# Head weights in pairs, a later load of y and later gated products in a hybrid S5 and attention block

## The chip, the core and the metric

The kernel runs on one core of a Trainium2 chip. The metric is the device time of one execution in microseconds (us). The engines work side by side, each through its own list of instructions in order: PE (TensorE, matrix products; PEld are its weight loads), DVE (VectorE), ACT (ScalarE), POOL (GpSimd), and SP (SyncE), which here issues nearly all transfers. An engine that waits for one instruction holds everything behind it.

## The reference

One decoder block over 1024 tokens of width 1024, in float32. What matters here is the first part: one normalised input `u` is projected to the input of a state-space branch, to queries, keys and values of 8 attention heads of width 64, to forget logits and to gates.

```python
u = rms_norm(h, norm_mix[l])
proj = u @ w_in[l]
u_ssm, q, k, v, f_logit, gate_logits = jnp.split(proj, [...], axis=-1)
y_ssm = jax.nn.gelu(s5_ssm(u_ssm, ...))
glu_a, glu_b = jnp.split(y_ssm @ w_glu[l], 2, axis=-1)
out_a = glu_a * jax.nn.sigmoid(glu_b)
att = forgetting_attention(q, k, v, f_logit + b_forget[l])   # causal, biased by summed log f
out_b = att @ w_fox_o[l]
h = h + (gate_a * out_a + gate_b * out_b) @ w_mix_out[l]
```

A cross-attention into 256 memory tokens, a gated FFN and a final norm follow.

## The kernel before

**Precision and stages.** Every float32 operand of a product is split into a high and a low part: ACT casts (`split`, line 178), DVE subtracts (line 179), and PE runs three products per tile pair (`mm3`, lines 168 to 170). The stages are the input with the norm, the state-space branch with the gates, the attention (class `Fox`), and the tail with the rest of the block. The attention stage runs from about 317 to 610 us and holds all of the change.

**Heads.** `Fox.run` loops over 8 heads and, in each, over 12 units: pairs of a block of 512 queries and a tile of 128 keys, numbered 0 to 11, units 0 to 3 for the first block and 4 to 11 for the second. `scores` issues a unit's products, the exponential on ACT (line 1627), and the split of the probabilities on ACT and DVE, or on DVE and POOL; `values_hi` and `values_lo` follow some units later. When the last unit of a head is summed, the first units of the next are under way: then `finish` fetches the head's denominators (`rc`, line 1663), DVE takes the reciprocals, and they go through DRAM (line 1665) and come back spread over 64 partitions (`rb`, line 1667). This last transfer is `self.spread`. `divide`, called in unit 4 of the next head, multiplies by it on DVE (line 1673), splits the result and stores it.

**Work beside the units.** `side[i]` lists what is issued with unit i of head h: in units 0 to 11 the projection of head h+2 (`part`, with the copies out of PSUM in `evac`), the row maxima of head h+1 (`row_max`, with `max_row` in unit 9, which sends the row by line 1610), the load of head h+3's query and key weights in unit 5 and their split in unit 9. In head 6 the y tiles, the output of the state-space branch, are loaded from DRAM (`load_y`: 8 calls of two transfers of 256 KB). In head 7 the `filler` is issued: loads of GLU weights and products with y, `Glu.values` for four blocks of 128 output columns.

**Buffers and order.** All weight loads, of the heads, of the GLU and of the later output projection, go through two buffers called `raw`, and their halves through four buffers each of `whi` and `wlo`. `raw` is free again when ACT and DVE have split it. The program order above is not the final one: a scheduler that models times moves instructions on each engine, so GLU weight loads (line 153) are issued on SP well ahead of head 7, from 506 us on, and loads of y (line 1698) from 526 us on, in head 5. `issue_after`, and `behind` on top of it, keep instructions from moving ahead of a named one. The GLU weights are first copied to `wg_d` in another order (line 1713).

**Pieces.** One head's queries take 64 columns of `w_in`, so a load of them consists of runs of 64 floats, 256 bytes.

Of the kernel before, what the change touches and what calls it, by code (L numbers as in the profile page):

```python
# [9 lines left out]
F32 = mybir.dt.float32  # L10
F32R = mybir.dt.float32r
# [8 lines left out]
P = 128  # L20
D = 1024
# [3 lines left out]
NH = 8  # L25
DH = 64
# [5 lines left out]
RAW = 1072  # L32

WSLOT = 1088
# [15 lines left out]
C_U, C_Q, C_K, C_V, C_G = 0, 512, 1024, 1536, 2056  # L50
# [16 lines left out]
def f32(ap):  # L67
    return ap.bitcast(F32)
# [26 lines left out]
def weave(main, side, lead=0):  # L95

    n, m, done = len(main) - lead, len(side), 0
    for i, f in enumerate(main):
        f()
        want = m if i + 1 == len(main) else max(0, (i + 1 - lead) * m // max(n, 1))  # L100
        while done < want:
            side[done]()
            done += 1
# [1315 lines left out]
class Fox:  # L1419
# [109 lines left out]
    def project(self, h):  # L1529

        B = self.B
        V, A, S = B.V, B.A, B.S
        K1, K2, Q1, Q2 = self.hb[h % 2]

        def load(behind=None):
            src = lambda c: self.w_in[:, c + h * DH:c + (h + 1) * DH].rearrange("(k p) c -> p k c", p=P)
            raw = self.raw[h] = B.wpool.tile([P, RAW], F32, tag="raw", bufs=2, name="raw")[:, :D]
            rv = raw.rearrange("p (k c) -> p k c", k=8)
            with B.behind(behind):
                S.dma_start(rv[:, :, 0:64], src(C_Q))  # L1540
                return S.dma_start(rv[:, :, 64:128], src(C_K))

        def parted(behind=None):
            wh = B.wpool.tile([P, WSLOT], F32R, tag="whi", name="whi")[:, :D]
            wl = B.wpool.tile([P, WSLOT], F32R, tag="wlo", name="wlo")[:, :D]
            with B.behind(behind):
                B.split(wh, wl, self.raw.pop(h))
            self.pj[h] = [t.rearrange("p (k c) -> p k c", k=8) for t in (wh, wl)]

        def part(hf, k):  # L1550
            if k == 0:
                self.pj[h, hf] = B.bank("mm")
            wh, wl = self.pj[h]
            rh, rl = self.uT.rhs(k, hf)
            B.mm3(self.pj[h, hf], wh[:, k, :], wl[:, k, :], rh, rl, k == 0, k == 7)

        def evac(hf):
            if hf == 1 and h > 1:
                self.gate_rows(h)
            ps = self.pj.pop((h, hf))  # L1560
            cs = slice(512 * hf, 512 * hf + 512)
            A.activation(Q1[0:64, cs], ps[0:64, :], AF.Copy, scale=0.125)
            A.copy(K1[0:64, cs], ps[64:128, :])
            V.scalar_tensor_tensor(out=Q2[64:128, cs], in0=ps[0:64, :], scalar=0.125, in1=f32(Q1[0:64, cs]),
                                   op0=ALU.mult, op1=ALU.subtract)
            V.tensor_sub(K2[0:64, cs], ps[64:128, :], f32(K1[0:64, cs]))
            A.activation(Q2[0:64, cs], ps[0:64, :], AF.Copy, scale=0.125)
            return A.copy(K2[64:128, cs], ps[64:128, :])

        return Projection(load, parted, [lambda hf=hf, k=k: part(hf, k) for hf in range(2) for k in range(8)],  # L1570
                          [lambda: evac(0), lambda: evac(1)])

# [113 lines left out]
    def run(self, y_d, yT, aT, w_glu, w_d, filler):  # L1686
        B, fp, S = self.B, self.fp, self.B.S
        self.aT = aT
        self.prepare_v()
        for t in range(NT):  # L1690
            self.values_of_v(1, t)
        self.log_forget()
        self.setup()

        def load_y(k, h):

            for i, dst in enumerate(yT.rhs(k, h)):
                S.dma_start(f32(dst).rearrange("p (t c) -> p t c", t=4),
                            y_d[k, i, 4 * h:4 * h + 4].rearrange("t p c -> p t c"))

        def load_att(k):
            for h in range(2):
                for i, dst in enumerate(aT.rhs(k, h)):
                    S.dma_start(f32(dst), self.att_d[i, k * P:(k + 1) * P, 512 * h:512 * h + 512])

        pro = [self.project(h) for h in range(NH)]
        for h in range(2):
            loaded = pro[h].load()
            pro[h].split()

        with B.tc.issue_after(loaded.ins):
            for k in range(4):
                S.dma_start(w_d[k].rearrange("(m g) c -> m g c", g=8),
                            w_glu[k * P:(k + 1) * P].rearrange("(g m) c -> m g c", m=16))
        for f in pro[0].parts[:8] + pro[0].evac[:1] + pro[0].parts[8:] + pro[0].evac[1:]:
            f()
        self.cumulate()
        for t in range(4):
            self.values_of_v(0, t)
        for h in range(2):  # L1720
            self.gate_rows(h)
        for f in pro[1].parts[:4]:
            f()
        weave(pro[1].parts[4:8] + pro[1].evac[:1] + pro[1].parts[8:], self.row_max(0))
        copied = pro[1].evac[1]()
        self.values_of_v(0, 4)
        self.max_row(0)
        pro[2].load()
        pro[2].split(copied)
        pro[3].load()  # L1730
        for t in range(5, 7):
            self.values_of_v(0, t)
        units = [(qc, kt) for qc in range(2) for kt in range(4 * qc + 4)]
        for h in range(NH):
            side = {i: [] for i in range(12)}
            late = h == NH - 2
            if late:
                for i, f in enumerate(pro[h + 1].parts[8:]):
                    side[i // 2].append(f)
                side[3].append(pro[h + 1].evac[1])  # L1740
            if h + 1 < NH:
                for i, f in enumerate(self.row_max(h + 1)):
                    side[(RSLOT_LATE if late else RSLOT)[i]].append(f)
                side[9].append(lambda: self.max_row(h + 1))
            if h + 2 < NH:
                n = 8 if h + 3 == NH else 16
                for i, f in enumerate(pro[h + 2].parts[:n]):
                    side[i if n == 8 else PSLOT[i]].append(f)
                side[9].append(pro[h + 2].evac[0])
                if n == 16:  # L1750
                    side[11].append(pro[h + 2].evac[1])
            if h + 3 < NH:
                side[9].append(lambda: pro[h + 3].split(self.exp))
            if h > 0 and h + 3 < NH:
                side[5].append(lambda: pro[h + 3].load(self.spread))
            if h == 0:
                side[0].append(lambda: self.values_of_v(0, 7))
            if late:
                for k in range(8):
                    side[4 + k].append(lambda k=k: load_y(k // 2, k % 2))  # L1760
            if h == NH - 1:
                for k in range(3):
                    side[6 + k].append(lambda k=k: load_att(k))
                for i, f in enumerate(filler):
                    side[i * 12 // len(filler)].append(f)
            for i, u in enumerate(units):
                self.scores(h, *u)
                for f in side[i]:
                    f()
                if len(self.hi_todo) > 2:  # L1770
                    self.values_hi()
                if len(self.lo_todo) > 1:
                    self.values_lo()
                if h and i == 4:
                    with B.tc.issue_after(self.mark.ins):
                        self.divide(h - 1)
        while self.hi_todo:
            self.values_hi()
        while self.lo_todo:
            self.values_lo()  # L1780
        self.divide(NH - 1)
# [29 lines left out]
```

## Time and profile before

| | us |
|---|---|
| median of 3 runs | 1593.38 (1593.16 to 1594.76) |
| the profiled execution | 1588.78 |
| its span | 1586.7 |

The mean granted clock of PE over the span was 0.988. A row of the timeline reads: start, duration, engine (`SPq` is SP issuing a transfer), line, operation, output<-input, sizes, and in brackets how long the engine stood before it and what ended that. In these rows raw<-in_w_in_dram in lines 1540 and 1541 is a head's load, raw<-wg_d a piece of GLU weights, yh and yl<-y_d a piece of y.

The wait list of PE between 300 and 680 us names ACT's `whi` (2.7 us, one time), ACT's exponentials (2.5 us, three times) and POOL's `pl` (1.5 us, one time) as the longest. From 580 us to 843 us no gap of PE above 0.2 us is in the trace.

### The profile page before, as it was taken

How to read it: one execution, taken by the hardware profiler on the slowest of the kernel's cores; microseconds unless marked ns; L12 is line 12 of the kernel's file. 1: busy time of each engine (PE TensorE's matmuls, PEld its weight loads, DVE VectorE, ACT ScalarE, POOL GpSimd, SP SyncE). 2: the span in 40 equal slices, each digit the busy share in tenths (PEclk: the TensorE clock that was granted, in tenths of full speed). 3: DMA queues.
4: the chain of work that ended last, by engine and by line, in shares of the span. 5: the costliest groups of instructions: out<-in, count | busy, mean ns of one | idle time of the engine just before them, and what ended most of it. 6: DMA issues, size and time to landing. Idle time of an engine off the chain costs nothing.

```text
span 1586.7 us, 20446 instructions
## 1 busy us (share of the span) xinstructions
PE 1534.0 (97%) x7313; PEld 1261.3 (79%) x7313; DVE 1019.5 (64%) x1850; ACT 655.2 (41%) x1173; POOL 254.3 (16%) x335
## 2 busy tenths in 40 slices
PE   7799999999999899999999999999999999999997
PEld 6578888898777668888888778888888888788885
DVE  6666445344688687675555697766677776565555
ACT  6422434323576553222435564333333333254342
POOL 2027653200212124110002200100000000000001
PEclk8899999999999999999999999999999999999999
DMA  7764445652023736357412186555444554796642
GB/s 266 125 132 80 127 131 110 130 145 30 18 52 48 186 95 208 125 172 259 160 46 75 54 283 239 170 164 163 155 153 160 166 162 156 261 391 223 195 150 106
DMA packets 197940, 240.86 MB, mean 152 GB/s; under 512 B 35448, under 2 KB 126488, under 8 KB 197328
## 3 DMA queue, kind: packets, MB, share of 16 engines
q1 hardware_dynamic: 191216, 223.84, 48.2%
q10 hardware_dynamic: 6624, 15.73, 2.6%
q8 instruction: 57, 0.93, 0.2%
q14 instruction: 43, 0.35, 0.1%
HBM read 165.60 MB, written 75.86 MB: 152 GB/s over the span
## 4 chain that ended last, share of the span: by engine, by line
PE 75%; DVE 8%; DMA 7%; issue 4%; POOL 3%; ACT 2%; SPq 1%; DVEq 0%; POOLq 0%; ACTq 0%
PE mm L868 14%; PE mm L168 7%; PE pv L868 7%; PE mm L170 7%; PE mm L169 7%; PE mm L1005 4%; PE sc L868 3%; PE sc L1005 3%; PE pv L1005 3%; PE sc L168 3%; PE sc L169 3%; PE sc L170 3%; DMA raw<-in_w_in_dram 2%; PE misc L1005 1%; PE pv L168 1%
## 5 line engine op out<-in xcount | busy, mean ns | idle before, releaser
L179 DVE TENSOR_TENSOR wlo<-raw,whi 128x1024 fp32r<-128x1024 f32 (+2 forms) x121 | 132.0, 1094 | 135.1 <-ACT whi L178 133.9
L178 ACT CAST whi<-raw 128x1024 fp32r<-128x1024 f32 (+2 forms) x124 | 116.1, 940 | 220.0 <-DMA raw<-in_w_ffn_in_dram 54.1
L168 PE MATMUL mm<-uh,whi 128*128 128x512 f32 x344 | 138.8, 404 | 2.8 <-ACT whi L178 2.7
L170 PE MATMUL mm<-uh,wlo 128*128 128x512 f32 x344 | 136.5, 397 | 1.7 <-DVE wlo L179 1.7
L169 PE MATMUL mm<-ul,whi 128*128 128x512 f32 x344 | 136.4, 396 | 0.0
L179 DVE TENSOR_TENSOR ol<-or,oh 128x1024 fp32r<-128x1024 f32 x73 | 89.3, 1224 | 71.6 <-ACT oh L178 70.3
L178 ACT CAST oh<-or 128x1024 fp32r<-128x1024 f32 x73 | 76.8, 1052 | 105.3 <-PE mm L1005 33.6
L900 POOL TENSOR_TENSOR g<-a,c 128x512 f32<-128x512 f32 x22 | 35.2, 1600 | 392.8 <-ACT a L899 373.9
L170 PEld LDWEIGHTS mm<-uh,wlo 128*128 128x128 f32 x344 | 65.7, 191 | 16.5 <-DVE wlo L179 3.1
L1630 POOL TENSOR_TENSOR pl<-pf,ph 128x512 fp32r<-128x512 f32 (+1 forms) x32 | 39.7, 1239 | 241.1 <-DVE ph L1629 196.1
L168 PEld LDWEIGHTS mm<-uh,whi 128*128 128x128 f32 x344 | 65.9, 192 | 15.5 <-ACT whi L178 3.2
L169 PEld LDWEIGHTS mm<-ul,whi 128*128 128x128 f32 x344 | 66.0, 192 | 11.3
L197 POOL TENSOR_TENSOR r<-ms,mhalf 128x1 f32<-128x1 f32 x26 | 15.1, 582 | 354.9 <-DVE ms L193 344.5
L1627 ACT ACTIVATE pf<-sc 128x512 f32<-128x512 f32 (+1 forms) x96 | 46.5, 490 | 46.3 <-DVE sc L1623 28.6
L868 PE MATMUL pv<-S3h,we 128*128 128x512 f32 x176 | 58.1, 389 | 0.0
L1633 DVE TENSOR_TENSOR pl<-pf,ph 128x512 fp32r<-128x512 f32 (+2 forms) x64 | 35.1, 550 | 10.2 <-ACT ph L1632 9.5
L1005 PE MATMUL mm<-oh 128*128 128x512 f32 x106 | 41.2, 389 | 0.0
L1005 PE MATMUL mm<-ol,oh 128*128 128x512 f32 x106 | 41.2, 389 | 0.0
L1005 PE MATMUL mm<-oh,ol 128*128 128x512 f32 x106 | 41.2, 389 | 0.0
L168 PE MATMUL mm<-yh,whi 128*128 128x512 f32 x104 | 40.9, 393 | 0.0
L168 PE MATMUL sc<-uh,whi 128*128 128x512 f32 x104 | 40.8, 393 | 0.0
L170 PE MATMUL mm<-yh,wlo 128*128 128x512 f32 x104 | 40.6, 390 | 0.0
(580 smaller groups left out, 4537.5 us busy)
## 6 DMA issues: line engine op xcount, KB each, us to landing
or<-c_d SPq DMA_DIRECT2D x77, 256.0 KB
raw<-in_w_in_dram SPq DMA_DIRECT2D x22, 512.0 KB
wo<-in_w_ffn_out_dram SPq DMA_DIRECT2D x22, 512.0 KB
c_d<-g SPq DMA_DIRECT2D x44, 256.0 KB
t_d<-wo SPq DMA_DIRECT2D x44, 256.0 KB
or<-t_d SPq DMA_DIRECT2D x44, 256.0 KB
raw<-in_w_ffn_in_dram SPq DMA_DIRECT2D x20, 512.0 KB
rawb<-in_w_ffn_in_dram SPq DMA_DIRECT2D x20, 512.0 KB
```

The source lines that it names most:

```text
L168: T.matmul(ps, lh, rh, start=first, stop=False)
L169: T.matmul(ps, lh, rl, start=False, stop=False)
L170: T.matmul(ps, ll, rh, start=False, stop=last)
L178: self.A.copy(hi, src)
L179: (self.G if pool_lo else self.V).tensor_sub(lo, src, f32(hi))
L197: self.G.tensor_tensor(out=r, in0=v, in1=self.mhalf[:, 0:n], op=ALU.pow)
L868: T.matmul(ps, l_[:, k, :], r_, start=first and k == 0 and i == 0, stop=k == 3 and i == 2, skip_group_check=True)
L900: G.tensor_mul(g[:, 512:], a1, c1)
L1005: T.matmul(ps, l_[:, gi], r_[:, 512:], start=n < 3 and p == 0 and k == 0 or n == 7 and p == 0 and k == 0, stop=p == NP - 1 and k == 2, ski ...
L1627: self.exp = A.activation(pf[:, off:], ps[:, off:], AF.Exp)
L1630: G.tensor_sub(pl[:, off:], pf[:, off:], f32(ph[:, off:]))
L1633: V.tensor_sub(pl[:, off:], pf[:, off:], f32(ph[:, off:]))
```

## The change

There are three parts. A head's query and key columns were loaded into one `raw` buffer by two transfers of 256-byte pieces. Now one load covers two heads: the queries of both into one buffer, the keys of both into the other, in 512-byte pieces, 512 KB each. Heads 0 and 1 are loaded at the start, 2 and 3 after the row maxima of head 0, 4 and 5 in unit 5 of head 1, 6 and 7 in unit 5 of head 3. The split takes each head's half out of both buffers, in two casts and two subtractions of 128x512 in place of one of 128x1024. The loads of y may not be issued before the latest `self.spread`. And the filler of head 7 begins in unit 2 instead of 0.

```diff
         def load(behind=None):
-            src = lambda c: self.w_in[:, c + h * DH:c + (h + 1) * DH].rearrange("(k p) c -> p k c", p=P)
-            raw = self.raw[h] = B.wpool.tile([P, RAW], F32, tag="raw", bufs=2, name="raw")[:, :D]
-            rv = raw.rearrange("p (k c) -> p k c", k=8)
+
+            self.raw[h // 2] = []
+            for c in (C_Q, C_K):
+                raw = B.wpool.tile([P, RAW], F32, tag="raw", bufs=2, name="raw")[:, :D].rearrange("p (k c) -> p k c", k=8)
+                self.raw[h // 2].append(raw)
+                with B.behind(behind):
+                    last = S.dma_start(raw, self.w_in[:, c + h * DH:c + (h + 2) * DH].rearrange("(k p) c -> p k c", p=P))
+            return last
+
+        def parted(behind=None):
+            self.pj[h] = [B.wpool.tile([P, WSLOT], F32R, tag=t_, name=t_)[:, :D].rearrange("p (k c) -> p k c", k=8)
+                          for t_ in ("whi", "wlo")]
+            o = h % 2 * DH
             with B.behind(behind):
-                S.dma_start(rv[:, :, 0:64], src(C_Q))
-                return S.dma_start(rv[:, :, 64:128], src(C_K))
-
-        def parted(behind=None):
-            wh = B.wpool.tile([P, WSLOT], F32R, tag="whi", name="whi")[:, :D]
-            wl = B.wpool.tile([P, WSLOT], F32R, tag="wlo", name="wlo")[:, :D]
-            with B.behind(behind):
-                B.split(wh, wl, self.raw.pop(h))
-            self.pj[h] = [t.rearrange("p (k c) -> p k c", k=8) for t in (wh, wl)]
+                for i, raw in enumerate(self.raw[h // 2]):
+                    B.split(*[t_[:, :, i * DH:(i + 1) * DH] for t_ in self.pj[h]], raw[:, :, o:o + DH])
...
             for i, dst in enumerate(yT.rhs(k, h)):
-                S.dma_start(f32(dst).rearrange("p (t c) -> p t c", t=4),
-                            y_d[k, i, 4 * h:4 * h + 4].rearrange("t p c -> p t c"))
+                with B.behind(self.spread):
+                    S.dma_start(f32(dst).rearrange("p (t c) -> p t c", t=4),
+                                y_d[k, i, 4 * h:4 * h + 4].rearrange("t p c -> p t c"))
...
+        loaded = pro[0].load()
         for h in range(2):
-            loaded = pro[h].load()
             pro[h].split()
...
         pro[2].split(copied)
-        pro[3].load()
...
-            if h > 0 and h + 3 < NH:
+            if h in (1, 3):
                 side[5].append(lambda: pro[h + 3].load(self.spread))
...
                 for i, f in enumerate(filler):
-                    side[i * 12 // len(filler)].append(f)
+                    side[2 + i * 10 // len(filler)].append(f)
```

In the changed kernel as scheduled, the GLU loads of the first four blocks are issued on SP between head 4 and the start of head 6, all y loads between the spread of head 5 and the denominators of head 6, and the first products with y keep their place in PE's list (unit 9 of head 6).

## The prediction

> **What bounds the kernel now.** I read the page first, then busy time in stretches of 20 us, then PE's timeline where PE was not full, then what released each gap.
>
> ```profile
> span 1586.7 us, 20446 instructions
> PE 1534.0 (97%) x7313; PEld 1261.3 (79%) x7313; DVE 1019.5 (64%) x1850; ACT 655.2 (41%) x1173; POOL 254.3 (16%) x335
> 350.00:360.00 10.00, 9.03 (x56) 7.50 (x55) 8.62 (x22) 4.55 (x8) 0.00 (x0) 1.00 0.03 10
> 480.00:500.00 20.00, 19.98 (x99) 15.09 (x96) 15.88 (x36) 13.56 (x25) 3.86 (x3) 1.00 0.40 67
> 520.00:540.00 20.00, 16.64 (x74) 12.39 (x75) 13.80 (x37) 12.71 (x25) 3.33 (x3) 0.91 0.61 168
> 540.00:560.00 20.00, 16.65 (x80) 11.29 (x79) 15.38 (x36) 13.04 (x26) 2.03 (x2) 1.00 0.72 182
> 560.00:580.00 20.00, 17.98 (x86) 12.77 (x84) 16.81 (x36) 10.67 (x20) 5.63 (x3) 1.00 0.44 119
> ```
>
> PE sets the pace: time is only won where PE stands or is throttled. The columns of a stretch are its length, then PE, weight loads, DVE, ACT and POOL, then clock, DMA share and GB/s. In the attention stage PE is full at head 3 (480 to 500), but loses 3.36, 3.35 and 2.02 us in 520 to 580 (heads 5 and 6), and 0.97 us in 350 to 360. These 9.7 us, and what the clock loses, are all that this change can win.
>
> ```profile
> 505.17 0.58 SPq L1540 DMA_DIRECT2D raw<-in_w_in_dram  x1
> 506.42 8.55 SPq L153 DMA_DIRECT2D raw<-wg_d  x2
> 521.54 1.04 ACT L178 CAST whi<-raw 128x1024 fp32r<-128x1024 f32 x1 [4.85 <-DMA raw<-in_w_in_dram]
> 522.64 0.50 PE L168 MATMUL mm<-uh,whi 128*128 128x512 f32 x1 [2.74 <-ACT whi L178]
> 523.90 0.50 PE L170 MATMUL mm<-uh,wlo 128*128 128x512 f32 x1 [0.53 <-DVE wlo L179]
> 524.58 0.33 PE L1645 MATMUL pv<-ph,vhi 128*65 128x256 f32 x1 [0.19 <-ACT ph L1632]
> 524.00:526.00 2.00, 1.81 (x7) 1.27 (x7) 1.67 (x4) 1.97 (x6) 0.00 (x0) 0.74 0.04 10
> 526.00:528.00 2.00, 2.00 (x8) 1.50 (x7) 1.70 (x4) 0.22 (x1) 0.00 (x0) 0.50 0.26 78
> 528.00:530.00 2.00, 2.00 (x10) 1.67 (x9) 0.44 (x2) 1.70 (x4) 0.00 (x0) 0.90 0.65 187
> 508.00:514.00 6.00, 6.00 (x29) 4.31 (x28) 5.71 (x11) 3.94 (x6) 1.29 (x1) 1.00 0.41 26
> ```
>
> The largest loss is one event. Head 7's weights were asked for at 505.17, two pieces of the GLU weights stood behind them, and from 508 to 514 the DMA engines moved only 26 GB/s. The weights landed near 521.5, 16 us after their issue; ACT, in order, waited 4.85 us, and PE lost 2.74 + 0.53 + 0.19 = 3.46 us. Then the clock fell: (0.26 + 0.50 + 0.10) x 2 us = 1.7 us more. **Together 5.2 us.**
>
> **The change part by part.** *Two heads in one load.* Heads 6 and 7 come together in head 3, heads 4 and 5 in head 1; the issue that was late is gone. Head 6's own load shows whether the earlier place holds twice the bytes.
>
> ```profile
> 480.36 0.58 SPq L1540 DMA_DIRECT2D raw<-in_w_in_dram  x1
> L178 ACT CAST whi<-raw x1: 1049/1049/1049, 491.9 to 491.9; 128x1024 fp32r<-128x1024 f32 x1
> q1 hardware_dynamic: 1277, 0.57, 87.8%
> q1 hardware_dynamic: 2087, 1.04, 90.2%
> ```
>
> From issue to cast there are 11.5 us. The last two rows are the DMA queue (packets, MB, share of 16 engines) in 481 to 486, where nearly all packets are 256-byte pieces of that load, and in 550 to 554, where they are 512-byte pieces of the GLU weights: 5 x 16 x 0.878 / 1277 = 55 ns a packet, against 4 x 16 x 0.902 / 2087 = 28 ns. One head has 2 x 128 x 8 = 2048 packets of 256 bytes, 2048 x 55 / 16 = 7.0 us; a pair has 2048 of 512 bytes, 2048 x 28 / 16 = 3.6 us. The pair should land near 486, nearly 6 us before its cast. Bounds: nothing won if head 7's cast meets another wait, 5.2 us at most. I take 5.0.
>
> The Trainium skill speaks against a price that falls with size: "DMA: Bandwidth & Descriptors", section "Why small descriptors are slow", gives a packet a fixed cost of about 3 cycles on top of its bytes (11 cycles at 256 bytes), by which 512 bytes would cost more per packet, an estimated 1.7 times. The trace disagrees, with 55 against 28 ns; by that rule the pair would take about 12 us and be slightly late at two casts, some 2 us off the gain.
>
> *The split in halves.* A cast and a subtraction of 128x1024 become two of 128x512 for each of 8 heads.
>
> ```profile
> 511.85 0.62 ACT L1632 CAST ph<-pf 128x512 fp32r<-128x512 f32 x1
> 522.62 1.22 DVE L179 TENSOR_TENSOR wlo<-raw,whi 128x1024 fp32r<-128x1024 f32 x1 [4.64 <-ACT whi L178]
> 531.30 0.68 DVE L1633 TENSOR_TENSOR pl<-pf,ph 128x512 fp32r<-128x512 f32 x1
> ```
>
> ACT: 2 x 0.62 - 1.04 = 0.2 us a head; DVE: 2 x 0.68 - 1.22 = 0.14. ACT and DVE have 6.4 and 4.1 us free in the 20 us of head 3 and hide it: zero. Bound without that cover: 8 x 0.2 = 1.6 us.
>
> *GLU pieces and raw slots.* Both raw buffers now hold a pair until its second head is split, so the first GLU piece waits on SP for head 7's split (cast at 516.7 or so). Queued behind it are the gate rows and the row of maxima for head 5, which in the old order wait for head 4's last scores, later than the split: no cost. But in the new order ACT casts GLU blocks 0 and 1 early in head 5, right after the exponential of its third unit, and three of their four pieces are issued behind the fetch of head 4's denominators.
>
> ```profile
> 529.60 0.54 SPq L1663 DMA_DIRECT2D rc<-num  x1
> 531.92 0.38 ACT L1627 ACTIVATE pf<-sc 128x256 f32<-128x256 f32 x1
> 548.81 2.08 SPq L153 DMA_DIRECT2D raw<-wg_d  x4
> ```
>
> That exponential ends 2.7 us after the fetch. Four pieces issued from 548.81 moved 1.04 MB by 554, so three need some 4.5 us: ACT waits 1 to 2 us, the exponential of the fourth unit behind it. PE has projections and maxima of other heads meanwhile; I charge 1.0 us (0 to 3).
>
> *y behind the spread.* Before, sixteen y pieces ran in head 5 from 526.20 on and slowed the spread of head 4's reciprocals.
>
> ```profile
> 526.20 0.39 SPq L1698 DMA_DIRECT2D yh<-y_d  x1
> 536.22 0.47 SPq L1667 DMA_DIRECT2D rb<-rd_d  x1
> 541.53 1.22 DVE L1673 TENSOR_TENSOR num<-num,rb 64x1024 f32<-64x1024 f32 x1 [1.60 <-DMA rb<-rd_d]
> 544.50 0.39 PE L1620 MATMUL sc<-hb,hb 69*128 69x256 f32 x1 [1.51 <-ACT pf L1627]
> 550.03 0.39 PE L1593 MATMUL mm<-hb,hb 68*128 68x256 f32 x1 [0.52 <-ACT hb L1568]
> ```
>
> The division stood 1.60 us on DVE, in front of everything, and PE 1.51, then 0.52 us near 550. Of these 2.0 us I take back 1.5 (0 to 2.0), since three GLU pieces now run ahead of that spread. The other 1.3 us of 540 to 560 stand at the start of head 6, where ACT has two GLU casts among its exponentials; one remains there: 0.7 (0 to 1.3).
>
> The price is paid in head 6. y is now issued only behind head 5's spread, and PE's new order puts the first y products at the same place as before, in unit 9 of head 6, not two units later: the scheduler moves them up to where it expects y.
>
> ```profile
> 560.79 0.46 SPq L1667 DMA_DIRECT2D rb<-rd_d  x1
> 566.90 0.50 PE L168 MATMUL mm<-yh,whi 128*128 128x512 f32 x1
> q1 hardware_dynamic: 3962, 2.11, 99.4%
> 574.92 0.44 PE L1652 MATMUL pv<-pl,vhi 128*65 128x512 f32 x1 [1.52 <-POOL pl L1630]
> ```
>
> PE reaches them 6.1 us after that spread's issue, and needs six pieces (y blocks 0 and 1) within 2 us. The queue row is 532 to 540: 2.11 MB in 8 us, 264 GB/s, or 1.0 us for a piece of 0.26 MB. With about 2 us to the first byte, the spread itself and one GLU piece ahead, the second piece lands 6 us after the issue, the sixth 10, against a need at 6 to 8. In the new order reciprocal and spread also stand behind the split of a GLU block, about 1 us later. PE should wait 2 to 3 us in bits; I take 2.5 (0 to 6). The later pieces stand behind the stores of head 5's result on SP, but their products are spread over 574 to 583: no further cost. Of the 1.9 us that PE lost at 573 to 578 to POOL and DVE I take 1.0 back, since these engines catch up while PE waits.
>
> *Forget gate.*
>
> ```profile
> 355.60 0.60 PE L1498 MATMUL misc<-ident,logf 128*8 128x128 f32 x4 [0.55 <-DVE logf L1485]
> 357.57 0.60 PE L1498 MATMUL misc<-ident,logf 128*8 128x128 f32 x4 [0.42 <-DVE cum L1499]
> ```
>
> The new loads let the scheduler put these transposes some 48 matmuls later, about 5 us, so both waits (0.97 us) go; the gate rows come later too, still ahead of their first use near 378. I take 0.8 (-1 to 1).
>
> Sum: 5.0 - 1.0 + 1.5 + 0.7 - 2.5 + 1.0 + 0.8 = **5.5 us won**. The profiled execution took 1588.8 us (span 1586.7 plus 2.1 around it), so 1583.3 there. The runs shown have a median of 1593.4, 4.6 us above it; taking the same difference off, 1587.9.
>
> **The rivals.**
> *The wait only changes its place (1591).* ACT stands for the GLU pieces in head 5 as it stood for head 7's weights. For: the same queue, the same in-order ACT, two casts in a row. Against: the pieces are 512 bytes, and the wait is 1 to 2 us against 4.85. If PE loses the full 3 us of the bound and y costs 3, 3.0 remain of the gain: 1590.4 to 1591.
> *y is late (slower, 1598).* The mechanism is SP: the spread, and with it y, stands behind two GLU pieces, the first of which waits for a raw slot. In the row at 506.42 two such pieces held SP for 8.55 us. If SP is held so long ahead of head 5's spread, PE pays each us of it, and a gap above 2.74 us brings the clock's 1.7: 8.55 + 1.7 - 5.5 = 4.8 us slower. It decides from a slip of 3.8 us on. For: the spread does stand behind two pieces. Against: no 256-byte load is in flight there.
> *The pair is late.* If a packet cost by its bytes, 110 ns, a pair would take 14 us and miss two casts by about 3 us each: 1594. The 28 ns speak against it.
> *All waits go (1582).* y is in time and the casts don't wait: 5.2 + 2.0 + 1.3 + 1.9 + 1.0 = 11.4. For: each gap has its cause in a queue that the change reorders. Against: y's margin is negative by the rows.
>
> **How the numbers follow.** The forecast has 0.50, with its own range 1584 to 1590.5; changed place 0.20; slower 0.13; pair late 0.03; all gone 0.14. What a measurement can tell is about 0.2%, 3.2 us: faster is below 1590.2, slower above 1596.6. Faster takes nearly all of the forecast, all of the best case and a little of the changed place: 0.63; slower the y case and a tail of others, 0.15; the rest, 0.22, is the same. The range, 1582 to 1595, reaches from the best case to where part of the y case is left out.
>
> **What would show it.** Right: no wait of ACT for raw near 517, full clock from 520 to 540, PE above 19 us in each 20 us of heads 4 and 5, a wait of PE on y from DMA in unit 9 of head 6 of 1 to 4 us in all, and no wait at the transposes of the forget gate. Wrong: a wait of ACT on the pair's loads in heads 1 and 3; a half clock in head 6 or 7; ACT idle above 3 us for a GLU piece in head 5; SP held for several us ahead of the spread of head 5.

## The result

The changed kernel takes 1599.18 us (median of 7, 1596.14 to 1600.62) against 1593.16 us before on the same chip, a ratio of 1.0036 with a 95% interval of 1.0024 to 1.0048: 0.36% slower by that ratio, 6.0 us by the two medians, where 5.5 us less were forecast. The profiled execution took 1600.62 us.

### The profile page after: what moved, and what is told of

It is laid out like the page before. It is cut to its first block, busy times and chain, and to the rows that moved or that the text cites. A ratio compares the mean times of both kernels' runs of the same rounds, so it can differ in the third digit from the quotient of the medians.

```text
span 1598.9 us, 20437 instructions
## 1 busy us (share of the span) xinstructions
PE 1539.4 (96%) x7313; PEld 1264.1 (79%) x7313; DVE 1019.7 (64%) x1858; ACT 656.3 (41%) x1181; POOL 254.7 (16%) x335
## 4 chain that ended last, share of the span: by engine, by line
PE 73%; DVE 9%; DMA 7%; issue 5%; POOL 3%; ACT 2%; SPq 1%; DVEq 0%; POOLq 0%; ACTq 0%
PE mm L868 15%; PE pv L868 7%; PE mm L168 6%; PE mm L169 6%; PE mm L170 6%; PE mm L1005 5%; PE sc L868 4%; PE sc L1005 4%; PE pv L1005 3%; PE sc L168 3%; PE sc L170 3%; PE sc L169 3%; DMA raw<-in_w_in_dram 2%; PE misc L1005 2%; DMA raw<-in_w_mem_kv_dram 1%
## 5 line engine op out<-in xcount | busy, mean ns | idle before, releaser
L179 DVE TENSOR_TENSOR wlo<-raw,whi 128x1024 fp32r<-128x1024 f32 (+1 forms) x129 | 134.1, 1044 | 135.5 <-ACT whi L178 130.7
L178 ACT CAST whi<-raw 128x1024 fp32r<-128x1024 f32 (+1 forms) x132 | 117.1, 895 | 223.1 <-DMA raw<-in_w_ffn_in_dram 53.2
L169 PEld LDWEIGHTS mm<-ul,whi 128*128 128x128 f32 x344 | 66.1, 192 | 11.4
L169 PE MATMUL mm<-yl,whi 128*128 128x512 f32 x104 | 41.0, 395 | 0.7 <-DMA yl<-y_d 0.7
L1100 POOL TENSOR_TENSOR sg<-sg,ga 128x512 f32<-128x512 f32 x16 | 29.9, 1891 | 72.6 <-DVE sg L1093 72.6
```

The source lines that it names most:

```text
L169: T.matmul(ps, lh, rl, start=False, stop=False)
L178: self.A.copy(hi, src)
L179: (self.G if pool_lo else self.V).tensor_sub(lo, src, f32(hi))
L1100: self.B.G.tensor_mul(self.out[j][:, cs], self.out[j][:, cs], ga)
```

## The profile after

The page, and busy time in stretches of 20 us as it was shown for the kernel before (length, then PE, weight loads, DVE, ACT, POOL, then clock, DMA share, GB/s). Line numbers are those of each run's own kernel, so a line that is L1593 before can be L1596 after. Three dots in a view stand for rows left out.

```profile
span 1598.9 us, 20437 instructions
PE 1539.4 (96%) x7313; PEld 1264.1 (79%) x7313; DVE 1019.7 (64%) x1858; ACT 656.3 (41%) x1181; POOL 254.7 (16%) x335
```

```profile
380.00:400.00 20.00, 16.12 (x81) 13.56 (x80) 9.87 (x28) 5.21 (x10) 0.00 (x0) 0.83 0.20 23
...
480.00:500.00 20.00, 20.00 (x99) 15.26 (x98) 16.15 (x41) 12.48 (x25) 3.75 (x4) 1.00 0.52 35
500.00:520.00 20.00, 16.56 (x78) 11.83 (x78) 12.30 (x37) 10.34 (x23) 2.89 (x3) 1.00 0.35 71
520.00:540.00 20.00, 19.94 (x98) 15.07 (x98) 15.19 (x36) 14.16 (x28) 2.57 (x2) 1.00 0.19 46
540.00:560.00 20.00, 17.23 (x78) 11.38 (x76) 18.04 (x44) 13.66 (x24) 4.63 (x4) 1.00 0.39 104
560.00:580.00 20.00, 17.45 (x79) 11.21 (x77) 17.32 (x39) 12.04 (x24) 3.31 (x3) 1.00 0.67 177
```

The stall of head 7's weights is gone: 520 to 540 is full, at full clock. Two new holes have opened ahead of it, at 380 to 400 (with the clock at 0.83) and at 500 to 520. The first, in the timeline, the two transfer queues and the clock:

```profile
371.32 1.02 SPq L1542 DMA_DIRECT2D raw<-in_w_in_dram  x2
372.60 0.35 SPq L1578 DMA_DIRECT2D hb<-cum_d  x1
...
375.70 2.10 SPq L1579 DMA_DIRECT2D hb<-cum_d  x1
...
384.04 1.64 PE L1596 MATMUL mm<-hb 68*128 68x128 f32 x4 [3.88 <-DMA hb<-cum_d]
```

```profile
q1 hardware_dynamic: 1130, 0.59, 88.1%
```

```profile
385.00:387.00 2.00, 2.00 (x6) 1.42 (x6) 1.66 (x6) 0.00 (x0) 0.00 (x0) 0.50 0.11 33
```

The load of heads 2 and 3 (1 MB) is issued right ahead of the four transfers of gate rows, 8 KB each. From 376 to 385 (the queue row: packets, MB, share of 16 engines) the DMA engines were 88% busy and moved 66 GB/s; the rows landed behind that, PE stood 3.88 us, and then ran at half clock. The second hole:

```profile
488.99 1.21 SPq L1542 DMA_DIRECT2D raw<-in_w_in_dram  x2
...
502.71 0.62 ACT L178 CAST whi<-raw 128x512 fp32r<-128x512 f32 x1 [1.92 <-DMA raw<-in_w_in_dram]
506.23 0.62 ACT L178 CAST whi<-raw 128x512 fp32r<-128x512 f32 x1 [2.90 <-DMA raw<-in_w_in_dram]
...
504.19 0.27 PE L1610 MATMUL misc<-ident,mc 128*8 128x128 f32 x1 [1.61 <-DVE mc L1608]
506.90 0.50 PE L168 MATMUL mm<-uh,whi 128*128 128x512 f32 x1 [1.14 <-ACT whi L178]
```

```profile
q1 hardware_dynamic: 695, 0.36, 101.5%
```

The pair of heads 6 and 7 was asked for at 488.99 and had landed only at 506, 17 us later (below, this slow phase of a load is called the crawl). ACT waited at both casts; DVE's subtractions behind them held the row maxima (L1608), and PE lost 1.61 us to those and 1.14 us to the weights. The queue row is 492 to 500: 695 packets in 8 us, 87 per us, each 8 x 16 x 1.015 / 695 = 187 ns. (The share adds up the time of all packets that began in the window, so it can pass 100%.)

The starts of PE's instructions show where whole kernels differ, also where single gaps are too short to be listed. For each matrix instruction I took the time to the next one's start, less the 10th percentile of that time for the same operation, tiles and shape over all kernels here, and summed it over the same stretch of PE's list. Every kernel has the same 7313 matrix instructions, and a stretch holds the same ones in all of them, but for one at an edge. Stretches are named by their times in the profile of before; each row is one profiled execution, in us lost:

```
                              350-395 395-485 485-515 515-530 530-590   whole
before                            5.1     5.7     1.7     6.3    10.7   101.8
after                            10.1     6.8     6.1     0.6    14.0   114.0
E5 after, once more               9.5     6.8     6.4     0.7    14.8   111.9
E1 gate rows first                6.9     6.8     6.4     0.7    13.2   109.9
E10 the same, once more           5.4     6.8     6.1     0.7    13.7   104.2
E2 pairs only                     9.9     6.8     6.0     0.7    12.6   107.5
E6 gate rows first, old y         5.3     6.8     7.5     0.7    10.9   105.6
E12 as E6, later filler           6.6     6.8     6.6     0.6    11.2   102.9
E11 as E6, y held                 6.9     6.8     6.4     0.7    13.3   106.7
E3 y and filler only              6.7     5.6     1.6     6.9    14.2   108.8
E4 pair 6, 7 earlier             10.4    18.1     3.2     0.6    13.6   117.5
E7 head 7 behind head 6           6.5     5.7     7.3     0.5    12.5   106.2
E8 columns of pairs exchanged     9.4    10.7     2.0     0.7    14.8   111.8
E13 columns of heads exchanged    6.4     5.8     4.3     0.5    11.7   102.4
E9 head 7 in halves               6.7     5.6     1.7     0.5    12.8    98.8
```

From before to after: 5.0 us lost at the gate rows, 1.1 in heads 0 to 2, 4.4 at the pair, 5.7 won at head 7's stall, 3.3 lost in heads 5 and 6; 8.1 us in these stretches. The whole differs by 12.2 us, as the two spans do (1598.9 and 1586.7). The other 4.1 us lie outside these stretches, where both kernels run the same instructions and where two executions of one kernel (after and E5) differ by up to 2.7 us in a single stretch of 100 us. The execution of before that was profiled was one of its faster ones inside the stretches too: E7, E9 and E13, which do the same work at the gate rows and in heads 5 and 6, lose 6.4 to 6.7 and 11.7 to 12.8 us there. Against their means (6.5 and 12.3) the change loses 3.6 us at the gate rows and 1.7 in heads 5 and 6, which makes 5.1 us in all, near the 6.0 of the medians.

## The experiments

Every kernel was timed beside the kernel before on its chip; ratios are against that. The theory: (A) most is lost by the gate rows behind a 1 MB load, (B) the rest by the late pair of heads 6 and 7. The rival: y behind the spread.

**E1, gate rows first.** `gate_rows` returns its last transfer, and

```diff
-            self.gate_rows(h)
+            gates = self.gate_rows(h)
...
-        pro[2].load()
+        pro[2].load(gates)
```

> The changed kernel, but the load of heads 2 and 3 may not be issued ahead of the four transfers of gate rows of heads 0 and 1. Theory A (most of the loss is the gate rows standing behind a 1 MB load that crawls at some 50 GB/s, with the half clock that follows the wait): no wait of PE for cum_d above 1 us, full clock from 380 to 400, some 5 to 7 us less than the changed kernel, so 1592 to 1594, about the kernel before. Theory B (the loss lies with the pair of heads 6 and 7 and in heads 5 and 6): under 2 us less, 1597 to 1599. If the load of heads 2 and 3 then lands too late for head 2's cast, a new wait of ACT for raw appears near 385 to 395 and the gain is halved.

1594.76 us (median of 5), ratio 1.0035 (1.0022 to 1.0049). Its timeline at the place:

```profile
371.62 0.22 SPq L1578 DMA_DIRECT2D hb<-cum_d  x1
...
372.87 1.02 SPq L1542 DMA_DIRECT2D raw<-in_w_in_dram  x2
...
380.24 0.44 PE L1596 MATMUL mm<-hb 68*128 68x384 f32 x1 [0.81 <-ACT hb L1571]
```

The wait of 3.88 us is gone (0.81 us for another cause stands in its place, as before the change), with the bytes of the load unchanged: A's mechanism is there. But the 5 to 7 us that theory A expected did not show in the time: the ratio did not move against the 1.0036 of the changed kernel, which had been timed on another chip. So the size needed more runs (E5, E6, E10).

**E2, pairs only.** In the changed kernel:

```diff
-                with B.behind(self.spread):
+                with B.behind(None):
...
-                    side[2 + i * 10 // len(filler)].append(f)
+                    side[i * 12 // len(filler)].append(f)
```

> The kernel before with the loads in pairs alone: y is not held behind the spread and the filler begins in unit 0. If the pairs carry the loss (A and B together): both the wait of 3.9 us for cum_d and the wait for the pair of heads 6 and 7 are there, and the time is 1598 to 1602. If y behind the spread or the later filler carries it: 1590 to 1594.

1595.97 us (6 runs), ratio 1.0040 (1.0026 to 1.0055). The time lies between the two ranges expected, but the kernel before was faster on this chip (1590.27 us), and by the ratio the pairs alone make the kernel slower by as much as the whole change. Both waits are there, 3.9 us for the gate rows and up to 2.6 us of ACT for the pair.

**E3, y and filler only**: these two hunks the other way round, in the kernel before.

> The kernel before with y behind the spread and the filler two units later, the head loads one by one as before. If the pairs carry the loss: not slower than before, 1590 to 1594, with the stall of head 7's weights near 521 still there, and heads 5 and 6 changed by under 2 us. If y carries the loss: 1597 to 1600, with waits of PE on y of over 3 us in head 6.

1595.06 us (5 runs), ratio 1.0035 (1.0021 to 1.0048). Slower too, against what I expected: the two halves of the change each cost what both cost together. They can, since the pairs win the 5.7 us of head 7's stall and lose more elsewhere, while E3 keeps that stall (6.9 us in 515 to 530). Heads 5 and 6 lost 3.5 us more than before, not under 2, of which waits of PE on y are 0.8 us.

**E4, the pair of heads 6 and 7 earlier.**

```diff
-                side[5].append(lambda: pro[h + 3].load(self.spread))
+                side[5 if h == 1 else 0].append(lambda: pro[h + 3].load(self.spread if h == 1 else None))
```

> The changed kernel, but the load of heads 6 and 7 is asked for in unit 0 of head 3 and without the spread, so that its query half leaves as soon as a raw buffer is free. Theory B (17 us from issue to landing, two casts late, their DVE halves and the row of maxima late with them): no wait of ACT for raw near 503 and 506, PE above 19.7 of 20 us in 500 to 520, and 2.5 to 3.5 us less than the changed kernel, 1595.5 to 1597. Theory A alone: no change, 1599, since these waits would be hidden. The wait for cum_d near 384 stays in both.

1605.55 us (4 runs), ratio 1.0103 (1.0087 to 1.0119): far worse than either expectation. The scheduler issued the first half at 474.26, just ahead of the row of maxima of head 3:

```profile
474.26 0.39 SPq L1542 DMA_DIRECT2D raw<-in_w_in_dram  x1
475.14 0.71 SPq L1613 DMA_DIRECT2D hb<-mr  x1
...
488.84 0.80 PE L1623 MATMUL sc<-hb,hb 69*128 69x512 f32 x1 [9.73 <-DMA hb<-mr]
```

A row of 4 KB took over 13 us behind the load, and PE stood 9.73 us. The casts of the pair no longer waited (ACT's rows show no idle time ahead of them, and 485 to 515 lost 3.2 us, not 6.1), so B stands; but what such a load costs is set by the small transfers issued behind it. It is the gate rows' accident at another place.

**E5, the changed kernel once more.**

> The changed kernel itself once more, beside the kernel before and the next kernels. Single times of one kernel lie up to 8 us apart, so what a part costs is read against this run. Expected 1.0036 (1.0025 to 1.005) of the kernel before. The waits that the first trace shows (near 384 for cum_d, near 503 and 506 for the pair) must be there again; the places of half clock need not.

1597.67 us (6 runs), ratio 1.0037 (1.0023 to 1.0051). The waits are there again: 4.1 us of PE for the gate rows, 2.9 us and 2.3 us of ACT for the pair.

**E6, gate rows first, y and filler as before**: E1 and E2 together, beside E5.

> The pair loads with the gate rows ahead of the load of heads 2 and 3, and with y and the filler as before the change. Theory: two causes, each about half. The gate rows cost 4 to 5 us, y and filler 2 to 4, the late pair 4, and the stall of head 7 that is gone gives 5 back. Then this kernel comes to 1.000 of the kernel before (0.998 to 1.002). Rival (y and filler cost nothing, the earlier run's 4.8 us was chance of the clock): as the run with the gate rows first alone, 1.0035.

1592.74 us (12 runs), ratio 1.0006 (0.9992 to 1.0019): the first expectation. Against E2, each by the kernel before on its chip, the gate rows are worth about 0.34%, from runs on two chips.

**E10 to E12, y or filler.** On one chip: E1 again; E1 with the second hunk of E2 (y held, filler from unit 0); E1 with its first hunk (y not held, later filler).

> The first experiment once more, on one chip with the next two: the pair loads with the gate rows ahead, y and filler as changed. Earlier 1.0035, and 1.0006 with y and filler as before. If y and filler cost what that says: 1.002 to 1.0035. If the earlier figure was high by chance: 1.0005 to 1.0015.

> Gate rows ahead, pair loads, y behind the spread, filler from unit 0. If y behind the spread is what costs in heads 5 and 6 (waits of PE on y near 575, 1.5 to 2.5 us in all): as the run before this one, 1.002 to 1.0035. If the later filler costs: 1.0005, as with both undone.

> Gate rows ahead, pair loads, y not held, filler from unit 2. If y behind the spread is what costs: 1.0005, as with both undone. If the later filler costs: 1.002 to 1.0035.

E10: 1594.74 us (12 runs), ratio 1.0021 (1.0010 to 1.0033), so the first figure of this kernel, 1.0035, was on the high side. E11: 1593.62 us (11 runs), 1.0021 (1.0011 to 1.0031). E12: 1591.17 us (11 runs), 1.0001 (0.9991 to 1.0012). Holding y costs some 0.2%, about 3 us; the later filler nothing. The traces show most of it: 13.7 and 13.3 us lost in heads 5 and 6 with y held (E10, E11), 10.9 and 11.2 without (E6, E12), 2.4 us apart. But only 0.9 us of that stands in listed waits of PE on y, where 1.5 to 2.5 were expected; E6 and E12 have no such wait. In E5 half clock came on top, at the very waits; its timeline and clock:

```profile
575.36 0.47 PE L168 MATMUL mm<-yh,whi 128*128 128x512 f32 x1 [0.26 <-DMA yh<-y_d]
576.17 0.50 PE L169 MATMUL mm<-yl,whi 128*128 128x512 f32 x1 [0.34 <-DMA yl<-y_d]
```

```profile
578.00:580.00 2.00, 2.00 (x7) 1.50 (x7) 0.28 (x1) 0.36 (x1) 1.28 (x1) 0.50 0.98 265
```

How often that happens over many executions no trace here tells. What makes up the rest of the 2.4 us stays open. The gate rows' share by E5 and E10 is 0.16%, by E2 and E6 0.34% (both across two chips, and the intervals of E5 and E10 overlap). In the table the five kernels with the wait for them lose 9.4 to 10.4 us in that stretch, the ten without it 5.1 to 6.9: on average 9.9 and 6.3, so 3.6 us or 0.23%, between the two.

**E7, head 7's load behind head 6's**, in the kernel before, by single heads.

```diff
-            if h > 0 and h + 3 < NH:
+            if h > 0 and h + 3 < NH - 1:
                 side[5].append(lambda: pro[h + 3].load(self.spread))
+            if h == 3:
+                side[10].append(lambda: pro[7].load())
```

> The kernel before with one edit: head 7's weights are asked for right behind head 6's, in head 3, by 256-byte pieces as before, and not in head 4. Same bytes at the same place as the pair, but head 6's pieces are first in the queue, and no larger load stands ahead of the gate rows. Theory B (the reads crawl, and what is cast first must not wait for the bytes of two heads): no wait of ACT for head 6's weights above 1 us, the stall of 2.7 us near 521 gone, 4 to 6 us less than the kernel before, 0.9965 to 0.9975. Rival (1 MB of these columns at this place costs the row of maxima its place whatever the order): PE loses 3 to 4 us near 495 to 500 and the time is 0.999 to 1.000.

1592.9 us (12 runs), ratio 1.0008 (0.9997 to 1.0019): near the rival's figure. The scheduler moved the load up to 483.34, as meant. Head 6's cast did not wait, but the row of maxima stood behind head 7's bytes:

```profile
496.31 0.71 SPq L1610 DMA_DIRECT2D hb<-mr  x1
...
503.24 0.80 PE L1620 MATMUL sc<-hb 69*128 69x512 f32 x1 [2.95 <-DMA hb<-mr]
```

PE lost 2.95 us there, about what the rival said. In all, 5.8 us are won at 515 to 530 and 5.6 lost at 485 to 515, without a pair. So the pair is not late for its 512-byte pieces; the bytes of head 7 cost this at this place in either form.

**E8, the columns of two pairs exchanged** (the loads of heads 4, 5 and of heads 6, 7 take each other's columns).

```diff
-... self.w_in[:, c + h * DH:c + (h + 2) * DH] ...
+... self.w_in[:, c + {4: 6, 6: 4}.get(h, h) * DH:c + ({4: 6, 6: 4}.get(h, h) + 2) * DH] ...
```

> The changed kernel with the columns of heads 4, 5 and of heads 6, 7 exchanged in their loads, so that the output is that of other weights; the transfers keep place, size and number. If the crawl belongs to the columns: the load in head 1 now moves at 40 to 50 GB/s for some 10 us and ACT waits there for raw, and the load in head 3 moves at 90 to 290 GB/s with no wait. If it belongs to the time or to what runs beside it: the load in head 3 crawls again, with waits of 1.9 and 2.9 us. One time, 1590 to 1602.

1598.34 us (one run). The crawl moved with the columns. ACT's timeline in head 1 and, in the last row, in head 3, where both casts of the pair now follow each other without a wait; then the queue from 440 to 448 (the load in head 1), then from 494 to 500 (the load in head 3):

```profile
450.59 0.62 ACT L178 CAST whi<-raw 128x512 fp32r<-128x512 f32 x1 [2.35 <-DMA raw<-in_w_in_dram]
453.40 0.62 ACT L178 CAST whi<-raw 128x512 fp32r<-128x512 f32 x1 [2.19 <-DMA raw<-in_w_in_dram]
...
502.47 1.14 ACT L178 CAST whi<-raw 128x512 fp32r<-128x512 f32 x2
```

```profile
q1 hardware_dynamic: 728, 0.37, 102.1%
```

```profile
q1 hardware_dynamic: 1480, 0.92, 94.5%
```

91 packets per us with columns 6 and 7, at 8 x 16 x 1.021 / 728 = 180 ns each; 247 per us and 61 ns with columns 4 and 5. In the table the loss has moved: against after, 395 to 485 lost 3.9 us more and 485 to 515 4.1 less.

**E13, the columns of single heads exchanged**, in the kernel before (256-byte pieces).

```diff
-            src = lambda c: self.w_in[:, c + h * DH:c + (h + 1) * DH]...
+            g = (0, 1, 3, 2, 1, 0, 7, 6)[h]
+            src = lambda c: self.w_in[:, c + g * DH:c + (g + 1) * DH]...
```

> The kernel before, in 256-byte pieces, with the columns exchanged: the load of head 2 takes those of head 3 and the other way round, 6 and 7 likewise, and the loads of heads 4 and 5 take those of heads 1 and 0; the output is that of other weights. In the kernel before the first 1024 packets of head 7's load (its queries, 507 to 516) moved at some 100 packets per us, the keys at 300. If slowness belongs to the columns: the load in head 3 (about 480, now head 7's columns) moves at about 100 packets per us for its queries and is late for its cast near 492, the load in head 4 (505, now head 6's) lands by 514 and the stall near 521 is gone; the first load, now head 3's, crawls ahead of the gate rows, so that PE waits for them by 1 to 3 us more near 377. If it belongs to the place: the load at 505 crawls again and the stall near 521 stays. One time, 1588 to 1598.

1589.37 us (one run, beside 1592.66 for before). ACT's timeline, and the queue from 484 to 490:

```profile
497.49 1.04 ACT L178 CAST whi<-raw 128x1024 fp32r<-128x1024 f32 x1 [3.69 <-DMA raw<-in_w_in_dram]
...
521.25 1.05 ACT L178 CAST whi<-raw 128x1024 fp32r<-128x1024 f32 x1
```

```profile
q1 hardware_dynamic: 627, 0.19, 42.3%
```

The load in head 3, with head 7's columns, is now the late one (3.69 us, 105 packets per us), the load in head 4, with head 6's, is in time, and the stall near 521 is gone. So the stall of the kernel before lay with head 7's columns, not with the place or with the GLU pieces in the queue. The last part of the expectation failed: with head 3's columns in the first load, PE waited at the gate rows no longer than before (0.82 and 0.62 us there, for other engines). So one head's bytes ahead of the gate rows did no harm here. But this is not the pair's case with fewer bytes: the rows had 12.6 us from their first issue (364.66) to the place where PE needs them (377.26), in the changed kernel 7.6.

**E9, head 7 in halves**, the version that this leads to, in the kernel before:

```diff
-        def load(behind=None):
+        def load(behind=None, halves="qk"):
...
-                S.dma_start(rv[:, :, 0:64], src(C_Q))
-                return S.dma_start(rv[:, :, 64:128], src(C_K))
+                if "q" in halves:
+                    last = S.dma_start(rv[:, :, 0:64], src(C_Q))
+                if "k" in halves:
+                    last = S.dma_start(rv[:, :, 64:128], src(C_K))
+                return last
...
-            if h > 0 and h + 3 < NH:
-                side[5].append(lambda: pro[h + 3].load(self.spread))
+            if h == 1:
+                side[5].append(lambda: pro[4].load(self.spread))
+            if h in (2, 3):
+                side[5].append(lambda: pro[7].load(pro[h + 3].load(self.spread), "qk"[h - 2]))
```

> The kernel before with one edit: head 7's query columns are asked for in head 2, behind head 5's load, its key columns in head 3, behind head 6's load; every place then carries one fast head and half of a slow one. Theory (head 7's columns move at some 100 packets per us wherever they stand, and what counts is that they are done before the row of maxima and the cast): no stall near 521, under 0.5 us of new waits in heads 2 and 3, 0.996 to 0.9975 of the kernel before. Rival (any byte behind the spread costs the rows their place): 2 to 4 us lost in heads 2 and 3, 0.999 to 1.001.

1586.26 us (11 runs), ratio 0.9967 (0.9957 to 0.9977): faster than both kernels. Its timeline on SP and ACT, and its stretches:

```profile
457.45 4.18 SPq L1543 DMA_DIRECT2D raw<-in_w_in_dram  x1
...
470.46 0.70 SPq L1615 DMA_DIRECT2D hb<-mr  x1
...
481.63 4.29 SPq L1545 DMA_DIRECT2D raw<-in_w_in_dram  x2
...
517.40 1.05 ACT L178 CAST whi<-raw 128x1024 fp32r<-128x1024 f32 x1
```

```profile
480.00:500.00 20.00, 20.00 (x100) 15.28 (x100) 16.18 (x36) 13.25 (x24) 3.86 (x3) 1.00 0.55 107
500.00:520.00 20.00, 19.97 (x98) 14.95 (x97) 17.64 (x46) 14.55 (x27) 4.60 (x4) 1.00 0.17 40
```

The queries' half leaves 13 us ahead of the row of maxima, the keys' half with head 6's load; no cast waits, nor does PE for a row, 5.8 of the 6.3 us in 515 to 530 are won, and nothing is lost ahead of them (5.6 and 1.7 us, as before). In heads 5 and 6 this execution lost 2.1 us more than that of before; the clock fell there (0.83 from 540 to 550), a loss of 1.7 us. The queue from 466 to 471, head 7's queries, and from 485 to 490, its keys and head 6's load:

```profile
q1 hardware_dynamic: 534, 0.14, 42.7%
```

```profile
q1 hardware_dynamic: 2121, 0.53, 84.7%
```

The queries move at 107 packets per us, the keys' stretch at 424.

## Why the prediction was wrong

**Forget gate: the step that failed first.** It was given +0.8 with bounds of -1 and 1, on the words that the gate rows "come later too, still ahead of their first use near 378". I looked at when they are issued, not at what is ahead of them and how long they then take. On SP before, and PE's first use of the rows:

```profile
362.97 0.40 SPq L1540 DMA_DIRECT2D raw<-in_w_in_dram  x1
...
364.18 0.69 SPq L1575 DMA_DIRECT2D hb<-cum_d  x1
...
376.77 0.39 PE L1593 MATMUL mm<-hb 68*128 68x128 f32 x2
```

In the old order head 2's 512 KB are ahead of the rows and head 3's load is behind them (365.92), in the new one 1 MB is ahead. And the rows have less time: 12.6 us from the first issue to the use before, 7.6 after (372.60 to 380.16, where PE's wait began), since the rows moved 8.4 us later and their use only 3.4. They took 11.4 us and landed at 384: a wait of 3.88 us where before two waits of 0.81 and 0.62 us for other engines stood, then half clock, 5.0 us lost by the two profiles, 3.6 by the averages over all kernels. With the rows put first that wait is gone (E1), though they have no more time there (371.62 to 379.03). So the load ahead of them is needed for the loss; whether it would have done harm with the old 12.6 us was not tried. Nor did the transposes stop waiting:

```profile
364.70 0.60 PE L1498 MATMUL misc<-ident,logf 128*8 128x128 f32 x4 [1.15 <-DVE logf L1485]
366.68 0.60 PE L1498 MATMUL misc<-ident,logf 128*8 128x128 f32 x4 [0.18 <-DVE cum L1499]
```

They lost 1.33 us after, 0.97 before.

**Two heads in one load: the gain right, the price wrong.** Of the stall at head 7 5.7 us came back, where 5.0 were taken. But "should land near 486, nearly 6 us before its cast" rested on 28 ns a packet, from pieces of the GLU weights, another tensor. The pair's packets took 187 ns in the crawl; it landed 17 us after its issue, not 5.6, late by 1.92 and by 2.90 us at two casts, and 4.4 us were lost. PE was busy for 16.56 of the 20 us from 500 to 520, where above 19 was foreseen. That is the rival "the pair is late", which the 28 ns had talked down to 0.03, though its reason, a cost by bytes, does not hold either (E8). The row to take was the one quoted for head 7's own load, 620 packets in 6 us: the reading that put it down to the place and the queue fell with E13. At that rate, 100 packets per us, the 1024 packets of a pair's queries alone take 10 us.

**The rule of the Trainium skill** in "DMA: Bandwidth & Descriptors", section "Why small descriptors are slow", that I set against it (a fixed cost on top of the bytes, an estimated 12 us for the pair) was nearer than my 3.6. Yet it does not describe this either: at one size, pairs move at 187 or at 61 ns a packet by their columns, and in the slow stretch 256 and 512 bytes move at nearly the same number of packets per us, 105 and 87.

**Split in halves, zero.** Every kernel with pairs lost 6.8 us in 395 to 485 (but for E4 and E8, which move a load or its columns there), every one with single heads 5.6 to 5.8. So the pairs cost 1.1 us in heads 0 to 2. Whether by the halves or by the order that they bring was not tried.

**y, GLU pieces and head 6.** Together they were put at -1.0 + 1.5 + 0.7 - 2.5 + 1.0 = -0.3; the two profiles have -3.3, and -1.7 against the mean of E7, E9 and E13. The first y products kept their place, and PE waited on y for 1.5 us, inside the 1 to 4 foreseen:

```profile
PE mm L168 <- DMA yh<-y_d: 0.8, 2, 0.6
PE mm L169 <- DMA yl<-y_d: 0.7, 2, 0.3
```

What was to come back for it, 3.2 us in all, did not on balance: the wait of 1.52 us for POOL is gone, that for ACT's exponential is there again (1.41 us, before 1.51), and by E10 to E12 holding y costs some 3 us. The term of 2.5 us for y began with "about 2 us to the first byte", which the trace of before does not show: its queue moved bytes 0.6 us after the issue at 505.17 and 1.2 us after the one at 560.79. The GLU pieces went as foreseen: ACT waited for them 0.76, 0.69 and 0.21 us in head 5. The rival in which SP is held ahead of that spread did not occur: SP issued each GLU piece there in under 1 us.

```profile
568.40 0.39 SPq L153 DMA_DIRECT2D raw<-wg_d  x1
...
569.37 0.43 SPq L153 DMA_DIRECT2D raw<-wg_d  x1
...
571.32 0.47 SPq L1670 DMA_DIRECT2D rb<-rd_d  x1
```

In sum the forecast's +5.5 became -8.1 us in the two profiles: 5.8 from the gate rows (0.8 to -5.0), 4.4 from the pair, 3.0 in heads 5 and 6 (-0.3 to -3.3), 1.1 in heads 0 to 2, less the 0.7 more that head 7 gave, make 13.6. Between the forecast and the two medians lie 11.5 us; the profile of before was a lucky one at the gate rows and in heads 5 and 6, as the table shows.

## What to carry to other kernels

Price a transfer by the same tensor and columns, not by the same piece size; a slow phase of one load that the trace of before already shows will come along when that load is moved. When a load is moved or doubled, list the small transfers that are issued in the 10 to 15 us behind it and what waits for them: they pay, not the load. And where a whole kernel wins and loses at several places, compare the time lost for the same work stretch by stretch before believing a median.

## What the runs showed of the hardware

- **Columns of one matrix differ.** The loads that hold head 7's columns of `w_in` move at 87 to 107 packets per us over windows of 5 to 8 us (after, before, E8, E13, E9), at whatever place they stand; at the same place as the pair of heads 6 and 7, that of heads 4 and 5 moves at 247 (E8). In E9 it is head 7's queries that crawl, not its keys. The slow rate is much the same for 256 and for 512 bytes, but the DMA engines are 42% busy with the one (E9, E13) and over 100% with the other. What in the addresses makes it so is open.
- **A row of 4 KB waits for what was issued ahead of it**: from its issue to its use over 13 us in E4, some 7 us in E7.
- **Half clock after the same waits is not the same each time**, and single executions of one kernel lay up to 8 us apart (before: 1585.79 to 1593.91 on one chip). PE has the same gaps near 377 in E9 and in E10; these two rows, of E9 and of E10, show the clock behind them. In E9 it is 0.96, 0.50 and 0.69 in the three stretches of 2 us from 378, a loss of 1.7 us, in E10 it stays at 1.00 (6.7 against 5.4 us in the table):

```profile
380.00:382.00 2.00, 2.00 (x7) 1.63 (x6) 1.20 (x5) 0.00 (x0) 0.00 (x0) 0.50 0.00 0
```

```profile
380.00:382.00 2.00, 2.00 (x11) 1.66 (x11) 1.51 (x5) 0.00 (x0) 0.00 (x0) 1.00 0.84 42
```
